# Layer 0's first modulation as plain fp32 products in four 32-column groups, its order of work, and where tiles start in SBUF

## The chip, the core and the metric

The kernel runs on one core of a Trainium2 chip. The metric is device time in microseconds (us) of one execution. Before the change three timed runs gave 1471.29, 1471.39 and 1478.82 us, median 1471.39. The engines are PE (TensorE; PEld is its weight load), DVE (VectorE), ACT (ScalarE), POOL (GpSimd, which issues one kind of DMA here) and SP (which issues the other).

## What is computed

Two layers of a hybrid backbone work on 256 latent and 256 context tokens of width 1024. Only the start of layer 0 is touched by most of the change:

```
mod = silu(c) @ w_mod[0] + b_mod[0]            # one row of 6*1024 for the latents (c), one for the context (c_ctx)
sh1, sc1, gt1, sh2, sc2, gt2 = split(mod, 6)
h  = rms_norm(x,   g_pre_mix[0]) * (1 + sc1)  + sh1
hc = rms_norm(ctx, g_pre_mix[0]) * (1 + csc1) + csh1
rq, rk, ... = split(h @ w_in[0], ...)          # the first 512 columns are rq and rk
```

Everything after it (retention, two attentions, merge, output projection, MLP, both layers) reads `h`.

## The kernel before

Activations are kept transposed, as eight chunks `hT` of 128 channels by 512 tokens (256 in most of layer 1), each as a rounded half and a remainder half in a fast fp32 form (`float32r`; hi and lo). Weights come as raw fp32 tiles of 128 x 1024 (512 KB each) on SP's queue; ACT casts a tile to its hi half (`wh`), DVE subtracts to get the lo half (`wl`), and each product is three matmuls: hi x hi, hi x lo, lo x hi (`mm3`). This goes for nearly every matmul of the kernel.

**The prologue** (function `prologue`, line 243) makes `sh1` and `sc1` of layer 0 and the first projection (512 columns of `w_in`, tiles `pr0` to `pr3`), in four quarters `kp` of 256 channels. A quarter has four pieces of `w_mod` (512 rows x 256 columns each) and one piece of `w_in`; all 20 pieces are loaded in that order (`load`, line 253), at most four ahead of the splits (`PLD`). Line 267 puts the halves of every third piece into the weight buffers and the others into general tiles. The letters of `PLAN` (line 55) are: `c` split pieces up to a number (ACT and DVE), `a` the modulation products of a quarter (line 285), `r` copy of the result row (line 296), `f` turn it into columns and make `sh1`, `sc1` (line 304), `t` transpose the normalised inputs of the quarter, `h` apply `sh1` and `sc1` and split (line 519), `g` the projection's products of the quarter (line 316). The silu vector, split into hi and lo, lies in `msr` as four columns of 128 stationary ones, so a modulation product is one matmul with the hi half of a piece and one with its lo half, each on 128 x 128 stationary and 256 moving columns: 32 matmuls a quarter.

While `Ordered.on` is set (line 325), PE, DVE and ACT instructions stay in the order of the text; after it a scheduler orders them. Waits between engines follow from the tiles. SP and POOL issue their DMAs in the order of the text too. `setup2` (line 1285), the first two tiles of the later vectors' `w_mod` (line 458) and two relative position tables (line 806) are POOL's, and nothing but a free tile holds them back.

**The other five vectors of layer 0 and all of layer 1** (`mod_dve`, line 401) are made on DVE: eight tiles of `w_mod` are scaled and added up (`acc`); the first addition reads the bias from the constant tile `brow`.

**SBUF.** General tiles are 4096 bytes a partition (pool `sp`, 31 of them), small ones 2048 (`tp`), weight halves 1056 numbers, 4224 bytes, in three buffers each (line 221). Two pad tiles (lines 114 and 120) set where the pools start. The built program puts general, small and raw tiles 256 bytes past a multiple of 512; the `wh` buffers 256, 384 and 0 past one, the `wl` buffers 128, 256 and 384.

Of the kernel before, what the change touches and what calls it, by code (L numbers as in the profile page):

```python
# [9 lines left out]
F32 = mybir.dt.float32  # L10
# [20 lines left out]
MLB = 2  # L31
NT = 8
NB2 = 5
C1 = 0
WR = 3
WH = 3
WLD = 3
# [10 lines left out]
XLATE = True  # L48
END = ((0, 0), (1, 0))
ORD = ((0, 4, 5), (0, 4, 8))  # L50
RW = 2
PLD = 4
# [29 lines left out]
def kernel(  # L82
# [121 lines left out]
    brow = const.tile([128, 2, 512], F32, tag="brow", name="brow")  # L204
# [36 lines left out]


    def prologue():
        pr = []
        M = {}
        raw, rdy = {}, {}
# [3 lines left out]
        mi = (0, 5, 10, 15)  # L250
        gi = (4, 9, 14, 19)

        def load(n):
            while len(raw) < min(n, len(wts)):
                i = len(raw)
                ap, k, *_ = wts[i]
                t = S("pr", F32) if i % RW else wrp.tile([128, 2, 512], F32, tag="wr", name="pr")
                raw[i] = t
                st["hold_sp"] = nc.sync.dma_start(
                    out=t.rearrange("p a b -> p (a b)").rearrange("p (k n) -> p k n", k=k), in_=ap)  # L260

        def cut(n):
            while len(rdy) < min(n, len(wts)):
                i = len(rdy)
                load(i + PLD)
                t, k = raw[i], wts[i][1]
                hi = wtile(whp, "wh", "pwh").rearrange("p (a b) -> p a b", a=2) if i % 3 == 0 else S("pwh")
                lo = wtile(wlp, "wl", "pwl").rearrange("p (a b) -> p a b", a=2) if i % 3 == 0 else S("pwl")
                st["hold_act"] = s_.copy(hi, t)
                st["hold"] = tt(lo, t, f(hi), ALU.subtract)  # L270
                rdy[i] = [u.rearrange("p a b -> p (a b)").rearrange("p (k n) -> p k n", k=k) for u in (hi, lo)]

        def init():
            msr = S("msr")
            v_.tensor_copy(msr[:, 0, :], brow[:, 0, :])
            v_.tensor_copy(msr[:, 1, :], brow[:, 0, :])
            msr = msr.rearrange("p a b -> p (a b)").rearrange("p (k m) -> p k m", k=8)
            v_.tensor_copy(msr[:, :, 0:2], cs)
            tt(msr[:, :, 2:4], cs, f(msr[:, :, 0:2]), ALU.subtract)
            M["msr"] = msr  # L280
            for n_ in ("sh1", "sc1"):
                st[0, n_] = smp.tile([128, 8, 2], F32, tag=n_, name=n_, bufs=2)
            pr.extend(mmt(f"pr{i}") for i in range(4))

        def mod(kp):
            ps = att("modps")
            for i in range(4):
                v, hf = i // 2, i % 2
                w = rdy[mi[kp] + i]
# [4 lines left out]
            M["ps", kp] = ps  # L294

        def row(kp):
            s_.copy(st["r5", kp][0:4, :], M["ps", kp][0:4, :])

        def bias(kp):
            r5 = st["r5", kp] = T("r5")  # L300
            nc.gpsimd.dma_start(out=r5[4:5, :].rearrange("o (v n) -> o v n", v=2),
                                in_=b_mod[0:1, 0:2 * D].rearrange("o (v n) -> o v n", v=2)[:, :, 256 * kp:256 * kp + 256])

        def fin(kp):
            r5 = st.pop(("r5", kp))
            pt = att("pm")
            for j in range(4):
                t_.matmul(pt[:, 2 * j:2 * j + 2], r5[0:5, 128 * j:128 * j + 128], sel[0:5, 18:20],
                          start=True, stop=True)
            p3 = pt[:, 0:8].rearrange("p (j e) -> p j e", e=2)  # L310
            hs = slice(2 * kp, 2 * kp + 2)
            v_.tensor_copy(st[0, "sh1"][:, hs, :], p3[:, 0:2, :])
            for s in range(2):
                stt(st[0, "sc1"][:, hs, s], p3[:, 2:4, s], 1.0, gp[:, 0, hs], ALU.add, ALU.mult)

        def gemm(kp):
            w_ = rdy[gi[kp]]
            for k in range(2):
                for i in range(4):
                    kc = 2 * kp + k  # L320
                    w = slice(128 * i, 128 * i + 128)
                    mm3(pr[i], (w_[0][:, k, w], w_[1][:, k, w]), hpair(kc, 512), kc == 0, kc == 7)

        def go(ws):
            Ordered.on = True
            load_x(4)
            load(PLD)
            for kp in range(2):
                bias(kp)
            init()  # L330
            sq = [pre_sq(0)]
            pre_xn(0, sq[0])
            sq.append(pre_sq(1))
            cut(C1)
            pre_xn(1, sq[1])
            for kp, plan in enumerate(PLAN):
                for c in plan.replace("_", " ").split():
                    o, n = c[0], int(c[1:])
                    if o == "c":
                        cut(n)  # L340
                    elif o == "a":
                        mod(n)
                    elif o == "r":
                        row(n)
                    elif o == "t":
                        ph = [pre_tr(n, s) for s in range(2)]
                    elif o == "f":
                        fin(n)
                        if n < 2:
                            bias(n + 2)  # L350
                    elif o == "h":
                        h32 = [T("h32") for _ in range(2)]
                        for j in range(2):
                            for s in range(2):
                                pre_h(0, 0, n, s, ph[s], (j,), h32[s])
                    elif o == "g":
                        gemm(n)
# [43 lines left out]
    def mod_dve(l, vec, streams):  # L401
# [53 lines left out]
        def step(kc):  # L455
            def go(ws):
                w = mrp.tile([128, 2, 512], F32, tag="mr", name="mr")
                nc.gpsimd.dma_start(  # L458
                    out=w, in_=w_mod[l, 128 * kc:128 * kc + 128, vec * D:vec * D + D].rearrange("p (a n) -> p a n", a=2))
                if kc == 0:  # L460
                    nc.gpsimd.dma_start(out=brow[0:1], in_=b_mod[l:l + 1, vec * D:vec * D + D].rearrange("o (a n) -> o a n", a=2))
                for s in streams:
                    if kc == 0:
                        st["acc", s] = S("acc", F32)
                    a = st["acc", s]
                    stt(a, w, cs[:, kc, s:s + 1], brow if kc == 0 else a, ALU.mult, ALU.add)
            return go

        fins = [fin1, fin2] if gate else [fin1, fin2, fin3]
# [257 lines left out]
    def attn_units(l, n, kind):  # L727
# [22 lines left out]
        def s1(hs, qb):  # L750
# [51 lines left out]
            def go():  # L802
                if na and qb == 0:
                    for h in hs:
                        bt = st["bt", h] = btp.tile([128, 384], F32, tag="bt", name="bt")
                        nc.gpsimd.dma_start(out=bt, in_=relb[l, h])
                context() if qb == 2 else latent()

            return go
# [464 lines left out]
    def setup():  # L1274
# [4 lines left out]
        v_.memset(brow, 0.0)  # L1279
# [5 lines left out]
    def setup2():  # L1285
# [7 lines left out]
        v_.tensor_copy(selr, sel4[0:4])  # L1293
        v_.memset(onesf, 1.0)
        v_.tensor_copy(ones, onesf)
        v_.tensor_copy(oneh[:, 0, :], brow[:, 0, 0:128])
        v_.tensor_copy(oneh[:, 1, :], brow[:, 0, 0:128])
        v_.tensor_copy(oneh[:, 0, 0:1], onesf[:, 0:1])
        v_.tensor_copy(oneh[:, 1, 1:2], onesf[:, 0:1])

# [202 lines left out]
```

## Time and profile before

| what | us |
|---|---|
| timed runs | 1471.29, 1471.39, 1478.82; median 1471.39 |
| the profiled execution | 1478.93 |
| its span, first to last instruction | 1477.2 |
| PE matmuls busy | 1427.6 (97%) |
| DVE, ACT busy | 1079.4 (73%), 747.1 (51%) |
| first product of the projection `pr` starts | 31.07 |
| first product of the next step (`pB`) starts | 72.69 |

Times in rows are us from the start of the span. A matmul's busy time is longer than the distance to the next start, because matmuls are pipelined; this text counts from start to start. The profiled execution lies 7.5 us above the median of the timed runs.

### The profile page before, as it was taken

Reading aid. Unit: us, or ns where it says so; the run is one execution under the profiler, and the core shown is the slowest. Engines: PE = TensorE matmul, PEld = TensorE weight load, DVE = VectorE, ACT = ScalarE, POOL = GpSimd, SP = SyncE. Lnnn points to the kernel's source line nnn. Section 1 sums busy time; section 2 is a strip of 40 time slices with the busy share of each in tenths; the row PEclk is TensorE's granted clock in tenths of the full one; section 3 lists DMA queues with packets and bytes.
Section 4 is the critical chain, followed back from the end, with each engine's and each line's share of the span. In section 5 each row is a group of like instructions: output and inputs, shape, how many; then the busy total and the mean of one; then the engine's idle time right before and its main releaser. Section 6 shows DMA issues by size and latency. Waiting matters only on the chain. (4 is left out here: it accounts for less than half of the span.)

```text
span 1477.2 us, 20910 instructions
## 1 busy us (share of the span) xinstructions
PE 1427.6 (97%) x7926; PEld 1212.9 (82%) x7926; DVE 1079.4 (73%) x1999; ACT 747.1 (51%) x1259; POOL 67.8 (5%) x131
## 2 busy tenths in 40 slices
PE   4999999999999999999999999999999999799997
PEld 4878788877788889988888887788889999699886
DVE  5785797787998669967755647986877886766544
ACT  5563565554323347625335155665546655576542
POOL 2000000000110000100001100000000000000000
PEclk9999999999999999999999999999999999899999
DMA  8622121222566556846546647443233445387653
GB/s 287 197 72 72 44 72 58 83 70 91 171 188 183 157 200 174 251 144 188 159 135 218 198 119 235 144 124 95 72 94 107 150 140 189 113 227 215 209 185 119
DMA packets 231957, 219.64 MB, mean 149 GB/s; under 512 B 7652, under 2 KB 188956, under 8 KB 231856
## 3 DMA queue, kind: packets, MB, share of 16 engines
q1 hardware_dynamic: 217856, 170.42, 37.4%
q0 software_dynamic: 14000, 47.88, 10.6%
q8 instruction: 62, 1.02, 0.3%
q14 instruction: 39, 0.32, 0.1%
HBM read 217.22 MB, written 1.05 MB: 148 GB/s over the span
## 5 line engine op out<-in xcount | busy, mean ns | idle before, releaser
L73 PE MATMUL ps<-hT,wh 128*128 128x256 f32 (+1 forms) x2480 | 602.4, 335 | 1.6 <-ACT wh L73 1.6
L73 ACT CAST wh<-wr 128x1024 fp32r<-128x1024 f32 x295 | 309.2, 1051 | 449.9 <-PE ps L73 180.9
L73 DVE TENSOR_TENSOR wl<-wr,wh 128x1024 fp32r<-128x1024 f32 x295 | 359.7, 1223 | 211.7 <-ACT wh L73 211.4
L73 PEld LDWEIGHTS ps<-hT,wh 128*128 128x128 f32 x2480 | 419.1, 190 | 55.5 <-issue 6.6
L73 PE MATMUL ps<-hT,wl 128*128 128x256 f32 (+1 forms) x1240 | 415.2, 335 | 5.1 <-DVE wl L73 4.9
L73 PEld LDWEIGHTS ps<-hT,wl 128*128 128x128 f32 x1240 | 234.9, 189 | 29.2 <-DVE wl L73 6.1
L73 PE MATMUL pO<-wh,u 128*128 128x512 f32 x768 | 241.7, 394 | 0.0
L73 PEld LDWEIGHTS pO<-wh,u 128*128 128x128 f32 x768 | 144.1, 188 | 33.7
L73 DVE SCALAR_TENSOR_TENSOR acc<-mr,cs,acc 128x1024 f32<-128x1024 f32 x112 | 141.2, 1282 | 28.9 <-DMA mr<-in_w_mod_dram 28.4
L73 PE MATMUL pO<-wl,u 128*128 128x512 f32 x384 | 151.2, 394 | 0.2 <-DVE wl L73 0.2
L73 PEld LDWEIGHTS pO<-wl,u 128*128 128x128 f32 x384 | 72.1, 188 | 16.6 <-DVE wl L73 0.6
L73 PE MATMUL pB<-wh,hT 128*128 128x512 f32 x256 | 82.9, 394 | 0.0
L458 POOL DMA_DIRECT2D mr<-in_w_mod_dram x80 | 42.6, 533 | 647.4 <-DVE acc L73 618.5
L73 PE MATMUL pO<-wh,yT 128*128 128x512 f32 x192 | 60.3, 393 | 0.0
L73 PEld LDWEIGHTS pB<-wh,hT 128*128 128x128 f32 x256 | 48.1, 188 | 10.6
L73 DVE TENSOR_TENSOR PT<-pt,PT 128x512 fp32r<-128x512 f32 x80 | 51.5, 682 | 2.8 <-ACT PT L73 2.2
L73 PE MATMUL pB<-wl,hT 128*128 128x512 f32 x128 | 50.3, 393 | 0.0
L73 ACT CAST PT<-pt 128x512 fp32r<-128x512 f32 x80 | 43.2, 599 | 8.5 <-PE pt L73 6.5
L73 PE MATMUL pt<-ident,P 128*128 128x128 f32 x320 | 42.0, 273 | 0.8 <-DVE P L73 0.6
L73 PEld LDWEIGHTS pO<-wh,yT 128*128 128x128 f32 x192 | 35.9, 188 | 8.2
L73 DVE TENSOR_TENSOR u<-rl,u 128x256 fp32r<-128x256 f32 (+1 forms) x71 | 36.7, 517 | 7.4 <-ACT u L73 7.4
L73 DVE TENSOR_SCALAR P<-P,su 128x512 f32<-128x512 f32 (+1 forms) x96 | 40.3, 440 | 1.6
(261 smaller groups left out, 1909.6 us busy)
## 6 DMA issues: line engine op xcount, KB each, us to landing
wr<-in_w_m_dram SPq DMA_DIRECT2D x143, 512.0 KB, 4.5
wr<-in_w_in_dram SPq DMA_DIRECT2D x104, 512.0 KB, 3.7
mr<-in_w_mod_dram POOLq DMA_DIRECT2D x80, 512.0 KB, 4.5
wr<-in_w_br_dram SPq DMA_DIRECT2D x24, 512.0 KB, 3.4
wr<-in_w_out_dram SPq DMA_DIRECT2D x24, 512.0 KB, 3.7
pr<-in_w_mod_dram SPq DMA_DIRECT2D x16, 512.0 KB, 6.3
bt<-in_relb_dram POOLq DMA_DIRECT2D x16, 192.0 KB, 2.7
X<-in_x_dram SPq DMA_DIRECT2D x4, 512.0 KB, 4.9
```

What stands on the lines that cost most here:

```text
L73: ins = call(*a, **k)
L458: nc.gpsimd.dma_start(out=w, in_=w_mod[l, 128 * kc:128 * kc + 128, vec * D:vec * D + D].rearrange("p (a n) -> p a n", a=2))
```

## The change

**The modulation products** read the raw fp32 pieces: no cast, no subtraction. The silu vector lies in `csz` as two columns of 32 per chunk; the four 128-row chunks of a piece go to four groups of 32 output columns (`ps[32 * k:...]`, 256 moving columns each), 16 matmul calls a quarter instead of 32 matmuls. `row` adds a bias tile on DVE, where ACT copied before; `fin` reads all 128 rows and a selector that adds the four groups. Only the four pieces of `w_in` are split, into the weight buffers.

**Loads.** All 20 pieces are issued at once, into general tiles and three raw ones. The bias rows are POOL's first loads after three constants. POOL then copies one number of piece 14 (`late`), and `setup2`, the later vectors' tiles and the position tables come behind that copy. `brow` is a general tile made anew for each vector, cleared by POOL.

**Order.** The products of quarter n come after the modulation of quarter n+1 from quarter 1 on. Five fp32 matmuls on a zero tile stand at PE's start.

**Places.** `PAD`, `PAD2` and the weight tiles' width (1152 numbers, 4608 bytes) change: general, small and raw tiles start at multiples of 2048 bytes, weight halves at multiples of 512.

```diff
-PAD, PAD2 = 16, 16
-PLAN = ["c4 t0 a0 c5 r0 f0 h0 c9 g0 c13",
-        "a1 t1 r1 c14 f1 h1 c18",
-        "a2 r2 c19 g1 t2 f2 h2",
-        "a3 t3 r3 c20 f3 h3 g2"]
+PLAN = "t0 a0 c0 r0 f0 d0 h0 g0 a1 r1 t1 c1 f1 d1 h1 a2 r2 t2 c2 f2 d2 h2 g1 a3 r3 t3 c3 f3 d3 h3 g2"
+GATE = 14
+PAD, PAD2, WP = 200, 272, 1152
+WARM = 5
...
-        t = pool.tile([128, 1056], F32R, tag=tag, name=name)
+        t = pool.tile([128, WP], F32R, tag=tag, name=name)
...
+        def load():
+            for i, (ap, k, *_) in enumerate(wts):
+                t = wrp.tile([128, 2, 512], F32, tag="wr", name="pr") if i % 5 == 4 and i < 15 else S("pr", F32)
                 raw[i] = t
+                st["hold_sp"] = nc.sync.dma_start(out=flat(t, k), in_=ap)
+                if i == GATE:
+                    st["late"] = nc.gpsimd.tensor_copy(out=late, in_=t[:, 0, 0:1])
...
         def init():
+            w, zero = att("warm"), T("zero")
+            v_.memset(zero, 0.0)
+            for _ in range(WARM):
+                t_.matmul(w, zero[:, 0:128], zero, start=True, stop=True)
+            t = S("csz", F32)
+            v_.memset(t, 0.0)
...
         def mod(kp):
-                    for p in range(2):
-                        t_.matmul(ps[:, 256 * v:256 * v + 256], M["msr"][:, 4 * hf + k, :], w[p][:, k, :],
-                                  start=(hf == 0 and k == 0 and p == 0), stop=(hf == 1 and k == 3 and p == 1))
+                    t_.matmul(ps[32 * k:32 * k + 32, 256 * v:256 * v + 256], M["csz"][:, 4 * hf + k, :], w[:, k, :],
+                              start=(hf == 0), stop=(hf == 1))
         def row(kp):
-            s_.copy(st["r5", kp][0:4, :], M["ps", kp][0:4, :])
+            r = M["r", kp] = T("r5")
+            tt(r, M["ps", kp], M["bias"][kp // 2][:, kp % 2, :], ALU.add)
...
-            with tc.issue_after(st["hold"].ins):
+            with tc.issue_after(st["hold"].ins), tc.issue_after(st["late"].ins):
                 setup2()
...
+                with tc.issue_after(st["late"].ins):
                     nc.gpsimd.dma_start(
                         out=w, in_=w_mod[l, 128 * kc:128 * kc + 128, vec * D:vec * D + D].rearrange("p (a n) -> p a n", a=2))
+                    if kc == 0:
+                        M["b"] = S("brow", F32)
+                        nc.gpsimd.memset(M["b"], 0.0)
+                        nc.gpsimd.dma_start(out=M["b"][0:1], in_=b_mod[l:l + 1, vec * D:vec * D + D].rearrange("o (a n) -> o a n", a=2))
```

PE's program, from its first instruction to the first products of the projection, before (`ph` transposes, `modps` modulation, `pm` is `fin`, `pr` the projection; numbers are buffers; 30 more rows of `modps` are left out):

```order
L73 MATMUL ph<-ident,X 128x128 x8
L73 MATMUL modps<-pwh,msr 128x256
L73 MATMUL modps<-pwl,msr 128x256
...
L73 MATMUL pm<-sel,r_138 128x2 x4
L73 MATMUL pr_149<-hT,pwh 128x512 x2
L73 MATMUL pr_149<-hT,pwl 128x512
```

The same place now, and on to the second quarter's modulation and the third's (15 rows of `pr` are left out):

```order
L69 MATMUL warm<-zero 128x512 x5
L69 MATMUL ph<-ident,X 128x128 x8
L69 MATMUL modps<-pr,csz 32x256 x16
L69 MATMUL pm<-csz,r_276 128x2 x4
L69 MATMUL pr_195<-hT,pwh 128x512 x2
...
L69 MATMUL modps<-pr,csz 32x256 x16
L69 MATMUL ph<-ident,X 128x128 x8
L69 MATMUL pm<-csz,r_345 128x2 x4
L69 MATMUL modps<-pr,csz 32x256 x16
```

The 32 matmuls of a quarter are 16 calls that read the raw piece, the run-up stands ahead of the first transposes, and the third quarter's modulation stands ahead of the second quarter's products.

DVE's program between the normalisation of the context and the second group of splits, before (`pwl` a lo half, `sh`, `sc` the columns of `fin`, `h` and `hT` step `h`):

```order
L73 TENSOR_SCALAR X<-X,py 128x1024 x2
L73 TENSOR_TENSOR pwl<-pr,pwh 128x1024 x5
L73 COPY sh_147<-pm 128x4
L73 SCALAR_TENSOR_TENSOR sc_148<-pm,gp 128x2 x2
L73 CAST hT<-h_283 128x256
L73 TENSOR_TENSOR hT<-h_283,hT 128x256
...
L73 TENSOR_TENSOR pwl<-pr,pwh 128x1024 x9
```

And now:

```order
L69 TENSOR_SCALAR X<-X,py 128x1024 x2
L69 TENSOR_TENSOR r_276<-modps,bias 128x512
L69 COPY sh_193<-pm 128x4
L69 SCALAR_TENSOR_TENSOR sc_194<-pm,gp 128x2 x2
L69 TENSOR_TENSOR pwl<-pr,pwh 128x1024
L69 CAST hT<-h_288 128x256
L69 TENSOR_TENSOR hT<-h_288,hT 128x256
```

Sixteen of 20 splits are gone; the one of the quarter stands between `sc` and the first cast of `hT`, and the addition of the bias stands ahead of `sh`.

## Rows read from the trace of the kernel before

**Rows 1.** The page's busy time, share and instructions of each engine.
```profile
PE 1427.6 (97%) x7926; PEld 1212.9 (82%) x7926; DVE 1079.4 (73%) x1999; ACT 747.1 (51%) x1259; POOL 67.8 (5%) x131
```

**Rows 2.** Waits of PE, whole run: waiter, tile, releaser: us, times, longest.
```profile
PE ph L73 <- DVE X L73: 14.2, 4, 10.4
PE ps L73 <- DVE wl L73: 4.9, 3, 2.7
```

**Rows 3.** Stretches: length, busy us of each engine, clock, DMA share, GB/s.
```profile
10.38:31.06 20.68, 12.58 (x48) 10.33 (x48) 11.01 (x29) 8.55 (x12) 1.77 (x4) 1.00 1.03 372
31.06:38.63 7.57, 7.57 (x24) 6.03 (x25) 7.50 (x11) 6.96 (x8) 0.00 (x0) 1.00 0.40 133
38.63:48.33 9.70, 9.70 (x82) 9.51 (x80) 6.65 (x14) 5.24 (x8) 0.00 (x0) 1.00 0.99 337
48.33:61.67 13.34, 13.34 (x90) 11.91 (x88) 9.41 (x20) 8.14 (x13) 0.00 (x0) 1.00 0.43 133
61.67:72.69 11.02, 11.02 (x50) 9.12 (x49) 9.99 (x37) 6.16 (x11) 1.01 (x2) 1.00 0.42 126
```

**Rows 4.** PE's timeline, quarter 0: start, length, tile, count, [idle before].
```profile
16.04 0.90 PE L73 MATMUL ph<-ident,X 128*128 128x128 f32 x3 [0.18 <-DVE X L73]
...
27.29 1.86 PE L73 MATMUL pm<-sel,r 5*128 5x2 f32 x8 [0.66 <-ACT r L73]
31.07 1.26 PE L73 MATMUL pr<-hT,pwh 128*128 128x512 f32 x2 [1.91 <-DVE hT L73]
...
33.83 1.05 PE L73 MATMUL pr<-hT,pwh 128*128 128x512 f32 x2
```

**Rows 5.** PE's timeline, quarter 1 to the end of the prologue.
```profile
38.63 0.28 PE L73 MATMUL modps<-pwh,msr 128*128 128x256 f32 x1
...
42.46 1.03 PE L73 MATMUL ph<-ident,X 128*128 128x128 f32 x8
43.42 1.05 PE L73 MATMUL pm<-sel,r 5*128 5x2 f32 x8
44.40 0.39 PE L73 MATMUL modps<-pwh,msr 128*128 128x256 f32 x1
...
48.33 0.62 PE L73 MATMUL pr<-hT,pwh 128*128 128x512 f32 x2
...
53.65 0.40 PE L73 MATMUL pr<-hT,pwl 128*128 128x512 f32 x1
62.48 0.62 PE L73 MATMUL pr<-hT,pwh 128*128 128x512 f32 x2
...
72.46 0.39 PE L73 MATMUL pr<-hT,pwl 128*128 128x512 f32 x1
72.69 0.39 PE L73 MATMUL pB<-wh,hT 128*128 128x512 f32 x1
```

**Rows 6.** ACT's timeline: the third and fourth input tile, the first piece.
```profile
8.10 1.06 ACT L73 ACTIVATE xj<-X 128x1024 f32<-128x1024 f32 x1 [0.35 <-DMA X<-in_xc_dram]
...
11.60 1.06 ACT L73 ACTIVATE xj<-X 128x1024 f32<-128x1024 f32 x1 [2.34 <-DMA X<-in_xc_dram]
...
13.89 1.04 ACT L73 CAST pwh<-pr 128x1024 fp32r<-128x1024 f32 x1 [1.15 <-DMA pr<-in_w_mod_dram]
```

**Rows 7.** DVE's groups from 0 to 72.69: count | busy, mean ns | idle before.
```profile
L73 DVE TENSOR_TENSOR pwl<-pr,pwh 128x1024 fp32r<-128x1024 f32 x20 | 23.5, 1220 | 7.9 <-ACT pwh L73 7.8
...
L73 DVE MEMSET brow<- 128x1024 f32 x1 | 0.9, 912 | 1.0 <-PEq L1492 1.0
```

**Rows 8.** PE's timeline: products on two different halves of the rows.
```profile
283.02 0.97 PE L73 MATMUL sl<-nk,nq 64*128 64x512 f32 x6
283.92 0.73 PE L73 MATMUL ps<-hT,wh 128*128 128x512 f32 x2
```

**Rows 9.** PE's groups by form, whole run: count | busy, mean ns.
```profile
L73 PE MATMUL ps<-hT,wh 128*128 128x512 f32 x1136 | 362.4, 398 | 0.0
...
L73 PE MATMUL ps<-hT,wl 128*128 128x512 f32 x568 | 226.3, 398 | 0.0
```

More of the change, by code (lines that the diff above doesn't have):

```diff
@@ L33 @@
 NB2 = 5
-C1 = 0
 WR = 3
@@ L203 @@
     cs = const.tile([128, 8, 2], F32, tag="cs", name="cs")
-    brow = const.tile([128, 2, 512], F32, tag="brow", name="brow")
+    late = const.tile([128, 1], F32, tag="late", name="late")
     ones = const.tile([128, 128], F32R, tag="ones", name="ones")
@@ L249, in prologue @@
         wts = md(0) + gm(0) + md(1) + gm(1) + md(2) + gm(2) + md(3) + gm(3)
[L250 to L257, printed above, removed]
-                raw[i] = t
-                st["hold_sp"] = nc.sync.dma_start(
-                    out=t.rearrange("p a b -> p (a b)").rearrange("p (k n) -> p k n", k=k), in_=ap)
@@ L262, in cut @@
[L262 to L271, printed above, removed]
@@ new lines, in cast, with cut, bias @@
+        def cast(kp):
+            hi[kp] = wtile(whp, "wh", "pwh").rearrange("p (a b) -> p a b", a=2)
+            st["hold_act"] = s_.copy(hi[kp], raw[5 * kp + 4])
+        def cut(kp):
+            lo = wtile(wlp, "wl", "pwl").rearrange("p (a b) -> p a b", a=2)
+            st["hold"] = tt(lo, raw[5 * kp + 4], f(hi[kp]), ALU.subtract)
+            rdy[kp] = [flat(u, 2) for u in (hi[kp], lo)]
+        def bias():
+            M["bias"] = [S("bias", F32) for _ in range(2)]
+            for i, t in enumerate(M["bias"]):
+                v_.memset(t, 0.0)
+                for kp in range(2):
+                    c = 512 * i + 256 * kp
+                    nc.gpsimd.dma_start(
+                        out=t[0:2, kp, :].rearrange("o (v n) -> o v n", v=2),
+                        in_=b_mod[0, 0:2 * D].partition_broadcast(2).rearrange("o (v n) -> o v n", v=2)[:, :, c:c + 256])
@@ new lines, in init @@
+        def init():
+            w, zero = att("warm"), T("zero")
[3 more added lines that the diff above has]
+            t = S("csz", F32)
+            v_.memset(t, 0.0)
+            M["csz"], M["selp"] = t[:, 0, 0:256].rearrange("p (k m) -> p k m", k=8), t[:, 1, 0:2]
+            v_.tensor_copy(M["csz"][:, :, 0:2], cs)
+            for j in range(4):
+                r = slice(32 * j, 32 * j + 2)
+                v_.tensor_copy(M["selp"][r, :], ident[r, r])
@@ L285, in mod @@
         def mod(kp):
-            ps = att("modps")
+            ps = M["ps", kp] = att("modps")
             for i in range(4):
                 v, hf = i // 2, i % 2
-                w = rdy[mi[kp] + i]
+                w = flat(raw[5 * kp + i], 4)
                 for k in range(4):
-                    for p in range(2):
-                        t_.matmul(ps[:, 256 * v:256 * v + 256], M["msr"][:, 4 * hf + k, :], w[p][:, k, :],
-                                  start=(hf == 0 and k == 0 and p == 0), stop=(hf == 1 and k == 3 and p == 1))
-            M["ps", kp] = ps
+                    t_.matmul(ps[32 * k:32 * k + 32, 256 * v:256 * v + 256], M["csz"][:, 4 * hf + k, :], w[:, k, :],
+                              start=(hf == 0), stop=(hf == 1))
         def row(kp):
-            s_.copy(st["r5", kp][0:4, :], M["ps", kp][0:4, :])
[L299 to L302, printed above, removed]
+            r = M["r", kp] = T("r5")
+            tt(r, M["ps", kp], M["bias"][kp // 2][:, kp % 2, :], ALU.add)
         def fin(kp):
-            r5 = st.pop(("r5", kp))
+            r = M.pop(("r", kp))
             pt = att("pm")
             for j in range(4):
-                t_.matmul(pt[:, 2 * j:2 * j + 2], r5[0:5, 128 * j:128 * j + 128], sel[0:5, 18:20],
-                          start=True, stop=True)
+                t_.matmul(pt[:, 2 * j:2 * j + 2], r[:, 128 * j:128 * j + 128], M["selp"], start=True, stop=True)
             p3 = pt[:, 0:8].rearrange("p (j e) -> p j e", e=2)
@@ L326, in go @@
             load_x(4)
-            load(PLD)
-            for kp in range(2):
-                bias(kp)
+            bias()
+            load()
             init()
@@ L333, in go @@
             sq.append(pre_sq(1))
-            cut(C1)
             pre_xn(1, sq[1])
[L336 to L357, printed above, removed]
+            ph = {}
+            for c in PLAN.split():
+                o, n = c[0], int(c[1:])
+                if o == "c":
+                    cast(n)
+                elif o == "d":
+                    cut(n)
+                elif o == "a":
+                    mod(n)
+                elif o == "r":
+                    row(n)
+                elif o == "t":
+                    ph[n] = [pre_tr(n, s) for s in range(2)]
+                elif o == "f":
+                    fin(n)
+                elif o == "h":
+                    h32 = [T("h32") for _ in range(2)]
+                    for j in range(2):
+                        for s in range(2):
+                            pre_h(0, 0, n, s, ph[n][s], (j,), h32[s])
+                elif o == "g":
+                    gemm(n)
             Ordered.on = False
             gemm(3)
-            with tc.issue_after(st["hold"].ins):
+            with tc.issue_after(st["hold"].ins), tc.issue_after(st["late"].ins):
                 setup2()
@@ L457, in go @@
                 w = mrp.tile([128, 2, 512], F32, tag="mr", name="mr")
[L458 to L461, printed above, removed]
+                with tc.issue_after(st["late"].ins):
+                    nc.gpsimd.dma_start(
+                        out=w, in_=w_mod[l, 128 * kc:128 * kc + 128, vec * D:vec * D + D].rearrange("p (a n) -> p a n", a=2))
+                    if kc == 0:
+                        M["b"] = S("brow", F32)
+                        nc.gpsimd.memset(M["b"], 0.0)
+                        nc.gpsimd.dma_start(out=M["b"][0:1], in_=b_mod[l:l + 1, vec * D:vec * D + D].rearrange("o (a n) -> o a n", a=2))
                 for s in streams:
@@ L805, in go @@
                         bt = st["bt", h] = btp.tile([128, 384], F32, tag="bt", name="bt")
-                        nc.gpsimd.dma_start(out=bt, in_=relb[l, h])
+                        with tc.issue_after(st["late"].ins):
+                            nc.gpsimd.dma_start(out=bt, in_=relb[l, h])
                 context() if qb == 2 else latent()
@@ L1295, in setup2 @@
         v_.tensor_copy(ones, onesf)
-        v_.tensor_copy(oneh[:, 0, :], brow[:, 0, 0:128])
-        v_.tensor_copy(oneh[:, 1, :], brow[:, 0, 0:128])
+        for i in range(2):
+            v_.tensor_scalar_mul(out=oneh[:, i, :], in0=onesf, scalar1=0.0)
         v_.tensor_copy(oneh[:, 0, 0:1], onesf[:, 0:1])
```

17 lines of the change are left out of this document (4 added, 13 removed).

## The prediction

> **What bounds the kernel now.** I read first the busy shares: PE matmuls 97% of the span, DVE and ACT far below [rows 1]. Time is lost only where PE waits or where its products are longer than they must be. The table of PE's waits, second, shows where it waits: the transposes `ph` for the normalised inputs `X`, 14.2 us in four waits, the longest 10.4; the largest later entry, products `ps` behind a lo half, is 4.9 [rows 2]. So the waiting that this change can touch is the prologue's. Third, the table by stretches: from 10.38 to 31.06 PE is busy 12.58 of 20.68 us and DMA is at its limit (1.03, 372 GB/s); from 31.06 to 72.69 PE is busy all the time (7.57 + 9.70 + 13.34 + 11.02), also in the stretch where DMA is at 0.99 [rows 3]. After 31.07 only less PE work can shorten the prologue; before it, what counts is how late the inputs, pieces and splits come.
>
> The clock column prints 1.00 for all these stretches, but durations tell two levels apart: the eight passes of `fin` take 1.86 at 27.29 and 1.05 at 43.42, two 512-column products 1.05 at 33.83 and 0.62 at 48.33 [rows 4, 5]. [...] PE comes to the upper level only after the gapless run that begins at 31.07; in the 61% busy stretch ahead of it it did not [rows 3, 4].
>
> **The change part by part.** The sum is made against the profiled execution, 1478.93 us, and then moved to the median.
>
> *Start of the projection.* The third input tile starts its square at 8.10, the context's second tile at 11.60 after a wait of 2.34 for its load [rows 6]. Earlier tiles come about 1.5 us apart, which is also 512 KB (0.524 MB) at 372 GB/s, 1.41 us [rows 3]. POOL's 2 MB of tiles and tables, which load at the same time before, now stand behind piece 14; so I put this tile at 9.6, 2.0 us earlier. The last transposes, which need it and run from 16.04 to 16.94 [rows 4], end then near 14.8. The first piece is cast at 13.89 now [rows 6]; the four of quarter 0 would land at 11.1, 12.5, 13.9 and 15.3, with no cast or subtraction between them and PE. POOL's bias rows are a few KB; ahead of the pieces they cost nothing that I can see.
>
> *The modulation products.* Before, quarter 1 has 32 passes from 38.63 to 42.46, 3.83 us, 0.12 each at the upper level [rows 5]. Now there are 16 calls. How often does PE pass for an fp32 call? `fin` has four fp32 calls and shows x8, two passes per call [rows 4, 5], so 32 passes of 256 columns again. What one takes is bounded from both sides. Below: the four column groups run fully beside each other, and a pass takes as long as 512 float32r columns, 0.23 us: 32 x 0.23 / 4 = 1.84 us a quarter. Above: no overlap, a full load of weights ahead of each pass (0.12, from `fin`, whose eight passes of two columns take 0.98 between 43.42 and 44.40 [rows 5], so are nearly all load) and the same 0.23: 32 x 0.35 = 11.2. The nearest row on overlap is the score products, on two halves of the rows: six in 0.90 us from 283.02 to 283.92, 0.15 each [rows 8], against 0.23 for one alone, so two groups gave 1.5 times, not 2. Four groups at 0.23 with an overlap of about 2 come to 32 x 0.12 = 3.84. I take that value: no gain in the products themselves.
>
> [...]
>
> *From the products to g0.* Transposes end at 14.8, products 3.84 us later at 18.6. The bias addition on DVE (512 elements from PSUM) I put at 0.7, near ACT's copy and the 0.66 that `fin` waited for it [rows 4]; `fin` takes 0.98; the stretch from its end (31.07 - 1.91 = 29.16) to the first product is 1.91 [rows 4]; and on DVE one split of 23.5 / 20 = 1.2 us [rows 7] now stands between `sc` and the first cast of `hT`. 18.6 + 0.7 + 1.0 + 1.9 + 1.2 = 23.4, with a little for queues 23.5. It was 31.07: 7.6 us less. The other 16 splits freed 19 us of DVE and about as much of ACT, but PE had no gap there, so I count them at nothing.
>
> *g0.* Its 24 products took 31.07 to 38.63, 7.56 us, the first half at the lower level [rows 3 to 5]; the same 24 take 48.33 to 53.65 plus one more, 5.55 [rows 5]. The five run-up products (fp32, 512 columns) start near 5.3, after DVE's clearing of two tiles (0.9 each by [rows 7]), and cost nothing: PE waits until 10.38 anyway [rows 2]. Whether they leave the clock high until g0 no row shows, since the transposes that follow are sparse. If it is high, g0 gains 2.0. If it is low, quarter 0's products take up to 2.9 more, `fin` 0.9 more, and g0 stays: 5.8 us lost of my sum. I take the upper level, since the low one needs gaps after a run like that of 31.07, and keep 5.8 for the range.
>
> *After g0.* The order a1, r1, t1, f1, a2, g1, a3, g2 has the same PE work: 41.6 us in all less 2.0. The last pieces must be there: at 1.41 us each from 9.6 on, the 19th and 20th land near 36 to 38; the held-back 2 MB, let go near 31, can push them by 2 / 0.372 = 5.4 us to about 43, and the products that need them (a3) begin 11.0 + 1.9 + 3.8 us ahead of `pB`, at about 46. Hidden; if it were not, up to 5 us. POOL's tiles come some 25 us later than before, but the first vector made of them is not read before the output projection, behind all of `pB`. The bias tile, cleared by POOL for each vector, takes the place of one that DVE cleared once, 0.9 us [rows 7]: nothing. Sum for the prologue: 7.6 + 2.0 = 9.6, minus 0.1 for three bias additions that PE meets no more than before: 9.5 us. `pB` starts near 63.
>
> *Places of tiles.* The same 512-column products run at two speeds. The second group of projection products, whose moving halves lie in the weight buffers, at other offsets from a multiple of 512 bytes than the stationary tiles, takes 23 steps from 48.33 to 53.65: 231.3 ns each. The third and fourth group, whose halves lie in general tiles at the same offset as the stationary ones, takes 44 steps from 62.48 to 72.46: 226.8 ns [rows 5]. The difference, 4.5 ns, is at the same clock and without waits. The later products `ps` read their halves from the weight buffers as the slow ones do; there are 1136 + 568 [rows 9], and 288 alike under `br`. After the change everything starts at a multiple of 512, so I expect the fast speed: 1992 x 4.5 = 9.0 us, at 97% busy nearly all of it in the end time. Bounds: the other 1824 products of this width (`pO`, `pB`, with weights stationary) may gain as much, 8.2 us more, or nothing (I take nothing, as no grouped row separates them); and if offset zero is a bad place in itself, 4.5 ns more on 1992, 9 us lost.
>
> [...]
>
> *Sum.* 9.5 + 9.0 = 18.5: 1478.93 - 18.5 = 1460.4 for a like execution. It stands 7.5 above the median; from the median, 1471.39 - 18.5 = 1452.9, so 1453.
>
> **The rivals.** One: places bring nothing; only the prologue's 9.5 is left, 1462. For it: 231 against 227 may come from DMA writes, 133 GB/s against 126 in the two stretches [rows 3]; against it, these shares are nearly alike.
>
> Two: column groups don't overlap, and the weight load stands in the open: 0.12 + 0.12 a pass, 7.7 us a quarter, four times 3.84 more: 1453 + 15.4 = 1468. For it `fin`'s passes, nearly all load [rows 5]; against it, a 32-column load is a quarter of the full one.
>
> Three, slower than before: loads in the open and fp32 columns at half rate, 0.35 a pass, 11.2 us a quarter, four times 7.36 more: 1453 + 29.4 = 1482. Place: the `modps` rows; it makes the kernel slower than before once a quarter takes more than 3.84 + 18.5 / 4 = 8.5 us. For it, that no row shows a wide fp32 product; against it, two overlapping groups of [rows 8].
>
> Four, better: groups fully beside each other (1.84 a quarter, 8 us less) and, or, `pO` and `pB` gaining too (8 less): 1437 to 1445, say 1442.
>
> That the change does not do what it says would be: the places come out of step for the halves, or the clock stays low in quarter 0 (both priced above).
>
> **How the numbers follow.** About 0.5%, 7.4 us, is what a measurement here can tell from no change: faster means below 1464.0, slower above 1478.8. Forecast 0.45 (own range 1446 to 1460, with the low clock, late loads, and part of the gains of rival four); rival one 0.20, rival two 0.10, rival three 0.08, rival four 0.17. Faster: the forecast, rival four, and three quarters of rival one (a quarter of it, with the low clock, lies at 1464 to 1468): 0.45 + 0.17 + 0.15 = 0.77. Same: 0.05 + 0.10 = 0.15. Slower 0.08. The range 1439 to 1468 leaves out rival three, the edge of rival two and the best end of rival four, together under 0.2.
>
> **What would show it.** `pB` starting near 63; first `pr` near 23.5, behind a `pwl` split; a quarter of `modps` from first to last start 3.8 us (1.8: four groups together; 7.7 or 11: rivals); the first two 512-column products of g0 at 0.62, not 1.05, for the clock; no wait of PE for a piece after g0; and later `ps` groups at 227 ns a product, not 231 to 233. The forecast is wrong if `modps` is longer than 8.5 us, if `ps` keeps its mean, or if PE waits for the last pieces near 46.

## The result, and the profile after

The changed kernel takes 1462.24 us (median of five, 1458.71 to 1464.21) against 1471.39 beside it (1470.72 to 1478.82): ratio 0.992, 95% interval 0.9898 to 0.9941, so 0.6 to 1.0% faster. 1453 was forecast, range 1439 to 1468. The sign and the range held; about half of the forecast 18.5 us came, or three quarters of it by the later runs of the kernel before (medians 1476.28 of 29, 1475.07 of 15, 1476.81 of 17).

The two profiled executions, 1478.93 and 1458.71, differ by 20.2 us. The page's busy times of the changed kernel, for [rows 1]:

```profile
span 1456.9 us, 20916 instructions
PE 1409.7 (97%) x7936; PEld 1200.3 (82%) x7936; DVE 1065.3 (73%) x1991; ACT 729.7 (50%) x1239; POOL 77.8 (5%) x142
```

PE's timeline of the prologue, for [rows 4, 5] (start, length, tile, count, idle before):

```profile
5.72 7.06 PE L69 MATMUL warm<-zero 128*128 128x512 f32 x10 [5.72 <-DVE zero L69]
...
14.28 0.55 PE L69 MATMUL ph<-ident,X 128*128 128x128 f32 x3 [0.33 <-DVE X L69]
14.76 1.93 PE L69 MATMUL modps<-pr,csz 128*32 128x256 f32 x32
17.51 1.05 PE L69 MATMUL pm<-csz,r 128*128 128x2 f32 x8 [0.81 <-DVE r L69]
20.94 1.25 PE L69 MATMUL pr<-hT,pwh 128*128 128x512 f32 x2 [2.38 <-DVE hT L69]
...
28.25 1.93 PE L69 MATMUL modps<-pr,csz 128*32 128x256 f32 x32
30.12 1.09 PE L69 MATMUL ph<-ident,X 128*128 128x128 f32 x8
...
37.09 1.02 PE L69 MATMUL pm<-csz,r 128*128 128x2 f32 x8 [2.08 <-DVE r L69]
37.97 1.09 PE L69 MATMUL pr<-hT,pwh 128*128 128x512 f32 x2
...
49.74 0.62 PE L69 MATMUL pr<-hT,pwh 128*128 128x512 f32 x2
...
59.94 0.39 PE L69 MATMUL pB<-wh,hT 128*128 128x512 f32 x1
```

The first `pB` starts at 59.94, 12.75 us earlier than in [rows 5]. A quarter's modulation takes 28.25 to 30.12, 1.87 us, where 3.84 were forecast: 0.058 a pass, the lower bound of the prediction's range. The first `pr` comes at 20.94, not 23.5. But `fin` of quarter 2 waits 2.08 for the bias addition, and g0 and g1 begin with pairs of 1.25 and 1.09 us, where a pair of the third group takes 0.62. The stretches of the two groups (length, busy us of PE, PEld, DVE, ACT, POOL; granted clock, DMA share, GB/s), for [rows 3]:

```profile
20.94:28.25 7.31, 7.31 (x24) 5.54 (x24) 1.67 (x5) 1.05 (x1) 0.00 (x0) 0.77 1.08 389
37.97:45.25 7.28, 7.28 (x27) 5.55 (x26) 3.94 (x12) 2.95 (x6) 0.00 (x0) 0.77 0.90 353
```

Their mean granted clock is 0.77: 0.55 and 0.54 up to 24.74 and 41.71, 1.00 behind. In g0 four products from 22.00 to 23.70 start 0.43 us apart and 14 from 24.74 to 27.93 start 0.23 apart. Each stretch takes 7.3 us, where 24 products at the upper level take 24 x 0.227 = 5.45. PE had idled 2.38 and 2.08 us shortly before. The input side went as forecast: ACT's timeline shows the fourth tile's square at 9.73 (11.60 in [rows 6], 9.6 forecast).

```profile
9.73 1.06 ACT L69 ACTIVATE xj<-X 128x1024 f32<-128x1024 f32 x1 [0.48 <-DMA X<-in_xc_dram]
```

From the first `pB` to the end of the span the profiles have 1477.2 - 72.69 = 1404.5 and 1456.9 - 59.94 = 1397.0 us: 7.5 less, 9.0 forecast. The two stretches, of before and of the change:

```profile
72.69:1477.20 1404.51, 1373.43 (x7639) 1165.99 (x7637) 1029.94 (x1872) 707.09 (x1203) 57.72 (x109) 0.99 0.47 144
59.94:1456.90 1396.96, 1361.47 (x7639) 1166.35 (x7637) 1030.06 (x1867) 708.38 (x1204) 68.10 (x120) 0.99 0.48 145
```

PE is busy 12.0 us less and idle 4.4 us more (31.1 and 35.5). So two things of opposite sign are in the 7.5. First, products are shorter. PE's groups by form, for [rows 9]:

```profile
L69 PE MATMUL ps<-hT,wh 128*128 128x512 f32 x1136 | 360.0, 396 | 1.8 <-ACT tg L69 1.0 <-DVE z L69 0.9
...
L69 PE MATMUL ps<-hT,wl 128*128 128x512 f32 x568 | 222.9, 392 | 0.0
```

Busy times overlap, so a stretch without waits is better: 192 products `pO` of the MLP of layer 0. Here are the second of them and the `ps` behind them, 191 steps, of before and of the change:

```profile
712.11 0.40 PE L73 MATMUL pO<-wl,u 128*128 128x512 f32 x1
...
756.40 0.63 PE L73 MATMUL ps<-hT,wh 128*128 128x512 f32 x2
```

```profile
695.80 0.39 PE L69 MATMUL pO<-wl,u 128*128 128x512 f32 x1
...
739.12 0.61 PE L69 MATMUL ps<-hT,wh 128*128 128x512 f32 x2
```

44.29 / 191 = 231.9 ns and 43.32 / 191 = 226.8 ns: the forecast's two speeds, but on `pO` too, which the sum had at nothing.

Second, waits came back. PE's waits that grew, for [rows 2], and the 300 us up to the same product at the end of layer 0's MLP, of before and of the change:

```profile
PE pO L69 <- DVE wl L69: 3.3, 2, 2.8
PE pm L69 <- DVE r L69: 2.9, 2, 2.1
PE pr L69 <- DVE hT L69: 2.4, 1, 2.4
```

```profile
615.40:915.40 300.00, 299.09 (x1303) 241.39 (x1302) 192.82 (x194) 113.93 (x151) 28.47 (x54) 1.00 0.57 179
```

```profile
600.00:900.00 300.00, 295.96 (x1307) 242.64 (x1305) 195.19 (x197) 115.10 (x154) 33.45 (x59) 0.99 0.59 180
```

PE is idle 0.9 us there before and 4.0 after. DVE's timeline of the changed kernel at the longest of these waits, and PE's behind it:

```profile
886.40 1.28 DVE L69 SCALAR_TENSOR_TENSOR acc<-mr,cs,acc 128x1024 f32<-128x1024 f32 x1 [0.46 <-DMA mr<-in_w_mod_dram]
890.30 1.29 DVE L69 SCALAR_TENSOR_TENSOR acc<-mr,cs,acc 128x1024 f32<-128x1024 f32 x1 [2.62 <-DMA mr<-in_w_mod_dram]
891.50 0.68 DVE L69 TENSOR_TENSOR z<-z,pO 128x512 f32<-128x512 f32 x1
892.10 1.22 DVE L69 TENSOR_TENSOR wl<-wr,wh 128x1024 fp32r<-128x1024 f32 x1
```

```profile
893.37 0.50 PE L69 MATMUL pO<-wl,u 128*128 128x512 f32 x1 [2.79 <-DVE wl L69]
...
896.15 0.63 PE L69 MATMUL pO<-wl,u 128*128 128x512 f32 x1
896.58 0.63 PE L69 MATMUL pO<-wh,u 128*128 128x512 f32 x1
```

PE's product behind that `wl` starts at 893.37 after 2.79 us of idle time. Then the clock falls too: eight products from 894.87 to 898.28 start 0.43 us apart and not 0.227, 1.6 us more, and the mean granted clock from 893.37 to 898.50 is 0.67. The lo half stands behind the last two additions of a modulation vector, and the second of these waits 2.62 for its tile. DVE's program order there, before and now:

```
L73 SCALAR_TENSOR_TENSOR acc<-mr,cs,acc 128x1024
L73 TENSOR_TENSOR u<-rl,u 128x512
L73 SCALAR_TENSOR_TENSOR acc<-mr,cs,acc 128x1024
L73 TENSOR_TENSOR wl<-wr,wh 128x1024
L73 TENSOR_TENSOR alo<-acc,ahi 128x1024
L73 TENSOR_TENSOR wl<-wr,wh 128x1024 x2
```

```
L69 TENSOR_TENSOR wl<-wr,wh 128x1024 x2
L69 SCALAR_TENSOR_TENSOR acc<-mr,cs,acc 128x1024 x2
L69 TENSOR_TENSOR z<-z,pO_7851 128x512
L69 TENSOR_TENSOR wl<-wr,wh 128x1024
```

Before, the three lo halves at the end come behind the last addition and without another between them; now two come ahead of the last two additions and the third waits for both. The scheduler made this order; the diff sets no order here. But the diff does change how these vectors get their bias (`brow`), besides the earlier end of the prologue, and no run separates which of the two moved the order.

### The profile page after: what moved, and what is told of

Its sections match the earlier page's. It is cut to its first block, busy times and chain, and to the rows that moved or that the text cites. A ratio compares the mean times of both kernels' runs of the same rounds, so it can differ in the third digit from the quotient of the medians.

```text
span 1456.9 us, 20916 instructions
## 1 busy us (share of the span) xinstructions
PE 1409.7 (97%) x7936; PEld 1200.3 (82%) x7936; DVE 1065.3 (73%) x1991; ACT 729.7 (50%) x1239; POOL 77.8 (5%) x142
## 3 DMA queue, kind: packets, MB, share of 16 engines
HBM read 217.23 MB, written 1.05 MB: 150 GB/s over the span
## 4 chain that ended last, share of the span: by engine, by line
PE 84%; DVE 8%; DMA 4%; issue 2%; ACT 1%; DVEq 0%; SPq 0%; ACTq 0%; POOLq 0%
PE ps L69 39%; PE pO L69 16%; PE br L69 7%; PE pB L69 6%; DMA mr<-in_w_mod_dram 3%; PE po L69 3%; PE pt L69 2%; DVE wl L69 2%; PE sl L69 2%; PE gkv L69 2%; PE pr L69 1%; PE ro L69 1%; DVE z L69 1%; DVE hT L69 1%; PE ph L69 1%
```

## Experiments

Each ratio is to the kernel before, run beside the experiment on the same chip. The changed kernel was not run beside them: a distance to its 1462.24 us lies between two sets of runs, and its ratio to compare with is 0.992 (0.9898 to 0.9941). "Tail" is the span less the start of the first `pB`, in the profiled execution; it was 1404.5 before and 1397.0 after.

**The kernel before once more.**

> The kernel before, unchanged, once more. Two accounts of why the two profiled executions differ by 20.2 us and the medians by 9.15. Account A: the first profile of before (1478.93) fell in an execution with some 7.5 us of extra waiting that has a place in the trace; then a second profile near 1471 has the same prologue (first pB at 72.7) and the same 512-column products (near 232 ns), and 7 us less somewhere behind it. Account B: the profile of before is typical and the timed runs of before are spread by something that the trace doesn't show; then a second profile at 1471 differs everywhere by 0.5%. Time by both: 1471 or 1478.

1475.23 us (12 runs) against 1476.28; profiled 1478.74. First `pB` at 72.50, tail 1477.0 - 72.50 = 1404.5, the same as in the first profile. That the totals agree is chance. The tail of this profile, and 170 to 190 us of the first profile and of this one:

```profile
72.50:1477.00 1404.50, 1376.51 (x7639) 1167.04 (x7637) 1029.78 (x1872) 706.67 (x1203) 57.74 (x109) 0.99 0.47 144
```

```profile
170.00:190.00 20.00, 20.00 (x93) 15.40 (x92) 16.81 (x39) 10.49 (x16) 0.00 (x0) 1.00 0.10 27
170.00:190.00 20.00, 20.00 (x64) 14.74 (x64) 10.73 (x26) 7.12 (x11) 0.00 (x0) 0.66 0.09 27
```

PE has no gap there in either, yet the granted clock is 1.00 in the first and 0.66 in this one, which falls some 6 us behind and makes it up later, with 28.0 us of idle time in the tail where the first has 31.1. So the accounts are not decided: the second profile did not fall near 1471 either, and 11 of the 61 later runs of the kernel before are as long. What it shows is that a tail from a single profile is good to a few us only, because the clock falls in other places in each of the two. The median of five, 1471.39, lay low: the 61 later runs have medians of 1475 to 1477. The spread goes with the clock: of 29 runs the shortest, 1469.02, had a mean granted clock of 0.991 and the longest, 1482.46, 0.984; correlation -0.87.

**Old places.**

```diff
-PAD, PAD2, WP = 200, 272, 1152
+PAD, PAD2, WP = 16, 16, 1056
```

> The changed kernel with the pads and the width of the weight tiles of before (16, 16, 1056); the instructions of every engine are the same in the same order. Theory P (places set the pace of 512-column products): products go back from 227 to about 232 ns, which is 13.7 us of flow by the two profiles; of it 6 us was given back in waits for late halves, so 7 to 14 us slower than the changed kernel, 1469 to 1476. Rival W (the gain behind the prologue comes from other waits, not places): within 2 us of 1462. The prologue ends near 60 to 61 by both.

1471.23 us (12 runs), 9.0 above the changed kernel, ratio to before 0.9967 (0.9946 to 0.9988). Tail 1469.4 - 61.13 = 1408.3, 11.3 more. The same 191 steps:

```profile
701.54 0.40 PE L69 MATMUL pO<-wl,u 128*128 128x512 f32 x1
...
745.84 0.63 PE L69 MATMUL ps<-hT,wh 128*128 128x512 f32 x2
```

44.30 / 191 = 231.9 ns: exactly the pace of before. (The pads put the general tiles at another offset than before, 288, but all distances between tiles modulo 512 are those of before.) Theory P holds, W falls. With these distances the tail is 3.8 us longer than before's 1404.5. PE is idle 34.4 us of it, against 31.1, so most of the 3.8 is waiting that the change brought.

**128 bytes apart, and 256.**

```diff
-PAD, PAD2, WP = 200, 272, 1152
+PAD, PAD2, WP = 232, 240, 1152      # 128 apart
+PAD, PAD2, WP = 264, 208, 1152      # 256 apart
```

> The changed kernel with general and small tiles 128 bytes past a multiple of 512, the weight halves still at multiples of 512; the order of all instructions is the same. Theory P: every 512-column product reads its moving tile and the next stationary one at places 128 bytes apart and takes 232 to 234 ns, 5 to 7 ns more on 3816 products, 19 to 27 us of flow, some of it hidden by waits: 1474 to 1488. Rival Q (only multiples of 2048, or the first tile's place, count, not the distance of the two): 1462, or no regular step.

> The changed kernel with general and small tiles 256 bytes past a multiple of 512 and the weight halves at multiples of 512; same order of all instructions. Theory M256 (what counts is whether the two tiles lie a multiple of 256 bytes apart): 227 to 228 ns a 512-column product, like the changed kernel, 1460 to 1464. Rival M512 (a multiple of 512 apart is needed): 231 to 233 ns as with 128 apart, 1470 to 1476.

128 apart: 1473.85 us (12 runs), 11.6 above the changed kernel; tail 1474.4 - 61.07 = 1413.3. 256 apart: 1458.76 (4 runs), no worse than the changed kernel; tail 1455.8 - 61.35 = 1394.5. The 191 steps, 128 apart, then 256:

```profile
702.83 0.39 PE L69 MATMUL pO<-wl,u 128*128 128x512 f32 x1
...
747.21 0.62 PE L69 MATMUL ps<-hT,wh 128*128 128x512 f32 x2
```

```profile
694.01 0.39 PE L69 MATMUL pO<-wl,u 128*128 128x512 f32 x1
...
737.33 0.61 PE L69 MATMUL ps<-hT,wh 128*128 128x512 f32 x2
```

44.38 / 191 = 232.4 and 43.32 / 191 = 226.8 ns. Over the whole tail PE is busy 1381.2 us at 128 and 1360.7 at 256, with the same instructions in the same order. M256 holds where all products have one distance: 0 and 256 are fast, 128 is slow. Neither the multiple of 2048 nor that of 512 is needed for it.

It does not hold product by product where distances are mixed. In the kernel before, by its places, `wh` lies 0, 128 or 256 bytes and `wl` 384, 0 or 128 past the other tile, so four of nine products are 128 apart (modulo 256). Were these alone slow, the mean would be 226.8 + 4/9 x 5.6 = 229.3 ns, and it is 231.9: even if the four take the 232.4 of the run with 128, the other five, 0 or 256 apart, take (9 x 231.9 - 4 x 232.4) / 5 = 231.5 on average, an estimate from the two means. So the distance within one product is not the whole cause; what else counts in such a stream, these runs leave open.

**No run-up.**

```diff
-WARM = 5
+WARM = 0
```

> The changed kernel without the five fp32 products at PE's start. Theory R (the run-up lifts the clock of quarter 0's modulation): its 32 passes take 3.7 us and not 1.87, fin 1.9 and not 1.05, first pB 2 to 3 us later, 1464 to 1465. Rival: the transposes lift the clock, or the end of the first products waits for pieces anyway; then within 0.5 us.

1462.03 us (6 runs), as with it. The trace is clearer:

```profile
10.32 0.48 PE L69 MATMUL ph<-ident,X 128*128 128x128 f32 x1 [10.32 <-DVE X L69]
...
14.93 2.99 PE L69 MATMUL modps<-pr,csz 128*32 128x256 f32 x32
18.75 1.05 PE L69 MATMUL pm<-csz,r 128*128 128x2 f32 x8 [0.82 <-DVE r L69]
```

The modulation takes 2.99 and not 1.93. The last three transposes ahead of it take 0.90 and not 0.55, `fin` behind it 1.05 as with the run-up, so the pace rises inside it. `pB` starts at 61.89, 1.95 later. Theory R is right in kind and too large (3.7, and 1.9 for `fin`, were expected). Two microseconds are below what these times tell, and the tails of single profiles differ by as much.

**One column group.**

```diff
-                    t_.matmul(ps[32 * k:32 * k + 32, ...], ..., start=(hf == 0), stop=(hf == 1))
+                    t_.matmul(ps[0:32, ...], ..., start=(hf == 0 and k == 0), stop=(hf == 1 and k == 3))
```

> The changed kernel with all 16 modulation calls of a quarter on one group of 32 output columns, accumulating one after the other, and fin over 32 rows; bytes, calls, passes and order are the same. Theory G (the four groups run beside each other; alone a pass of 256 fp32 columns takes 0.23 us): modps of a quarter goes from 1.87 to 32 x 0.23 = 7.4 us, 5.5 more in each of four quarters, of which quarter 0 may hide a little behind late pieces: first pB near 80, time near 1482 to 1485. Rival H (a pass takes 0.06 by itself, groups or not): 1.9 a quarter, 1462. Between, 0.12 a pass: 3.8 a quarter, pB near 68, 1470.

1473.62 us (10 runs), 11.4 above the changed kernel (the profiled executions, 1474.77 and 1458.71, differ by 16.1). PE's timeline and its first `pB`:

```profile
33.27 7.09 PE L69 MATMUL modps<-pr,csz 128*32 128x256 f32 x32
40.30 1.09 PE L69 MATMUL ph<-ident,X 128*128 128x128 f32 x8
...
77.04 0.39 PE L69 MATMUL pB<-wh,hT 128*128 128x512 f32 x1
```

7.03 us a quarter, 0.22 a pass, 5.16 more than with four groups, and `pB` is 17.1 later. Theory G holds: a pass of 256 fp32 columns costs what 512 float32r columns cost (0.22 and 0.227 us here), and four groups run 7.03 / 1.87 = 3.8 times faster than one.

**g1 ahead of fin 2.**

```diff
-... a2 r2 t2 c2 f2 d2 h2 g1 a3 ...
+... a2 r2 t2 c2 g1 f2 d2 h2 a3 ...
```

> The changed kernel with the projection products of quarter 1 ahead of fin 2 instead of behind it (modulation and transposes of quarter 2 stay ahead). [...]

Without the wait of 2.08 at `fin` 2 and the 1.8 us of g1's slow start `pB` would come near 56, an estimate from 59.94. It starts at 59.79, as with the change: the wait is gone at `fin` 2 and stands at `fin` 3, and slow pairs stand in g2 (1.06 us at 48.73 and at 50.01).

```profile
40.45 0.95 PE L69 MATMUL pm<-csz,r 128*128 128x2 f32 x8
...
46.26 1.02 PE L69 MATMUL pm<-csz,r 128*128 128x2 f32 x8 [1.98 <-DVE r L69]
```

So the edit moved the wait and did not remove it. The median, 1456.92 (4 runs), is still 5.3 below the changed kernel's, with a tail of 1395.3 against 1397.0; the ratios, 0.9884 (0.9863 to 0.9904) and 0.992, overlap in their intervals. That difference is not in the edited stretch. Of the 1.7 us between the tails 1.1 lie at 140 to 148 us, where the granted clock is 0.79 here and 0.57 in the changed kernel's profile; where the rest comes from the runs don't settle.

**No gate.**

```diff
-                    st["late"] = nc.gpsimd.tensor_copy(out=late, in_=t[:, 0, 0:1])
-            with tc.issue_after(st["hold"].ins), tc.issue_after(st["late"].ins):
+            with tc.issue_after(st["hold"].ins):
...
-                with tc.issue_after(st["late"].ins):
```

> The changed kernel with POOL's loads not held behind piece 14; the four bias loads then come behind the tables and the first vector tile in POOL's queue. Theory L (2 MB of early loads delay inputs and biases): the fourth input tile lands 2 us later, the bias addition of quarter 0 waits, first pr 2 to 5 us later than 20.9, pB 62 to 65, 1464 to 1467. Rival: PE is bound by the order of its own work, pB within 0.5 us of 59.9, 1462.

1467.54 us (6 runs), ratio 0.9947 (0.9925 to 0.9969), which overlaps with the changed kernel's; the trace is clearer, with `pB` at 67.64. ACT's fourth input tile comes at 12.85 and not 9.73, and PE waits for pieces in quarter 0:

```profile
12.85 1.06 ACT L69 ACTIVATE xj<-X 128x1024 f32<-128x1024 f32 x1 [2.01 <-DMA X<-in_xc_dram]
```

```profile
21.40 1.08 PE L69 MATMUL modps<-pr,csz 128*32 128x256 f32 x8 [1.38 <-DMA pr<-in_w_mod_dram]
```

Theory L holds, at 7.7 us of `pB` and not 2 to 5. Three of them are the input (the last transposes start at 17.29 and not 14.28) and 2.1 waits for pieces. Most of the rest is the clock, which is 0.52 from 18.00 to 32.22: `fin` takes 1.86 there and not 1.05.

**The later vectors spread over three steps fewer**, in the changed kernel and in the one before.

```diff
-MLB = 2
+MLB = 5
```

> The changed kernel with the steps of the later modulation vectors spread over three steps fewer of the MLP of layer 0, so that on DVE no addition of a vector stands between the last lo halves of the MLP; the prologue is untouched. Theory B (order on DVE: lo halves queue behind an addition that waits for its load; PE waits 3 to 5 us some 830 to 848 us after the first pB in all four profiles with the changed order, and 0 to 1.1 in the two of before): these waits go, 3 to 5 us less, 1457 to 1459. Rival C (the waits come from the loads themselves, whatever the order): they stay, 1462.

> The kernel before with the vectors spread over three steps fewer, as in the run that did this to the changed kernel. Theory B (the change of order spoilt a place that was good before): the two profiles of before have 0 to 1.2 us of long waits there, so little to win, 0 to 2 us below before. Rival (fewer steps help whatever the order): 5 to 8 us below before, as for the changed kernel.

In the changed kernel: 1453.44 us (4 runs), ratio to before 0.985 (0.9828 to 0.9872); tail 1450.1 - 59.91 = 1390.2, 6.8 less. In the one before: 1473.83 (12 runs), ratio 0.9984 (0.9967 to 1.0); tail 1475.8 - 70.97 = 1404.8, as without the edit. The 300 us at the end of the MLP, in the changed kernel with the edit:

```profile
600.00:900.00 300.00, 300.00 (x1339) 246.93 (x1338) 199.17 (x202) 118.33 (x157) 33.44 (x59) 1.00 0.60 184
```

No idle time is left. Theory B holds: in the kernel before, idle 0 to 0.9 us there, the edit is worth 0 to 5 us by the interval, in the changed kernel more. Of the 6.8 us of the tail 5.0 are idle time of PE (35.5 us without the edit, 30.5 with it). The rest is busy time: 1.6 are the slow products behind the long wait, and 1.1 at 140 to 148 us are none of the edit's doing, since the granted clock is 0.57 there in the changed kernel's profile and 0.79 in this one; about 1 us is lost again elsewhere.

**Both together**, with the split of a quarter's `w_in` piece on DVE ahead of `fin`'s results.

```diff
+PLAN = "t0 a0 c0 r0 d0 f0 h0 g0 a1 r1 t1 c1 d1 f1 h1 a2 r2 t2 c2 d2 g1 f2 h2 a3 r3 t3 c3 d3 f3 h3 g2"
+MLB = 5
```

> The kernel of the run with the vectors spread over fewer steps, and in the prologue the split of each quarter's w_in piece on DVE ahead of fin's results instead of behind them, and g1 ahead of fin 2. Theory D (split behind fin's results holds the first product back): first pr at 19.6 and not 20.8, the wait at fin 3 about 1 us and not 2, pB near 57.5, 2 to 3 us less than that run: 1450 to 1452. Rival: waits move again, pB near 59.8, 1453.

1451.46 us (6 runs, 1448.23 to 1460.25), ratio to before 0.9851 (0.9817 to 0.9885): the fastest version here, though not clearly apart from the one without the new order.

```profile
20.53 0.96 PE L69 MATMUL pr<-hT,pwh 128*128 128x512 f32 x2 [1.98 <-DVE hT L69]
...
45.49 1.02 PE L69 MATMUL pm<-csz,r 128*128 128x2 f32 x8 [1.56 <-DVE r L69]
...
57.35 0.39 PE L69 MATMUL pB<-wh,hT 128*128 128x512 f32 x1
```

`pB` is at 57.35 as expected, but the first product came only 0.4 earlier, not 1.2: the wait for `hT` is 1.98 with the split out of its way and was 2.38 with it, so most of the split had lain beside the chain from `fin` over `h` to `hT`.

## Why the prediction was right or wrong

**Wrong: the start from the median.** The step "from the median, 1471.39 - 18.5" failed. The profile of before was a long run, but no stray: the later medians are 1475 to 1477, and from those the change brings 13 to 15 us. The rest of the distance to the profiles' 20.2 is chance on both sides: 2 to 4 us by which the profile of before lies above those medians, and 3.5 by which the changed kernel's lies below its own.

**Luck: the sum.** The sum for a like execution was 1460.4 and the profiled one took 1458.71. But that is not its terms coming true: 7.9 us in the modulation and 7.3 in `pO` and `pB`, which it did not have, were for the most part lost again in waits and at the lower clock level, which it did not have either. So both mechanisms of rival four came true (1.87 a quarter, `pO` and `pB` faster) without its 1437 to 1445, and the time of rival one, 1462, came true without its mechanism.

**Right in sign, 3.3 us too small: the prologue.** Forecast 9.5, measured 12.75. The failing term is the modulation: 1.87 a quarter and not 3.84, since four column groups run beside each other almost fully (one group alone takes 7.03 a quarter, 3.8 times as long); I had carried the 1.5 of the score products [rows 8] over as 2. Rivals two and three fall with it: `modps` was to take 7.7 or 11. The loads that they put in the open run beside products on the same rows, in the kernel before too: from 31.06 to 38.63 the loads are busy 6.03 of 7.57 us while products on all 128 rows never pause [rows 3]. A 32-column load takes 109 ns on average in the changed kernel and a full one of `fin` 191, so more than a quarter of it; a pass with its load takes 0.058 us. Of the 4 x 1.97 = 7.9 us that the groups won in the modulation, part was lost again: 2.1 at `fin` 2, which the prediction said would not happen ("three bias additions that PE meets no more than before"), and 1.8 each in g0 and g1, which it had put at the upper level. That leaves 2.2 of the 3.3; the last 1.1 are small steps of both signs. The value 5.5 for g0 was wrong; the reason for doubt, sparse work on PE ahead of it, was there. The reason given for the upper level, that the low one needs gaps, does not hold in general: the second profile of before ran at 0.66 from 170 to 190 us without a gap, the changed kernel's at 0.57 from 140 to 148.

**Right: loads.** The fourth input at 9.73 (9.6 forecast), no wait for a piece, run-up hidden: the last transposes start at 14.28 with it and 14.10 without. The gate is worth the 7.7 us of `pB` that its absence cost.

**Right in kind, wrong account: places.** 9.0 forecast, 7.5 in the tail. Counted over all 512-column steps without a gap behind the first `pB`, `ps` and `br` gain 4.2 ns each, 8.3 us, near the 9.0; but `pO` and `pB`, which I had at nothing, gain 4.0 ns each, 7.3 us more. Waits (4.4) and, as far as they were traced, stretches at the lower clock took half of the 15.6 back. By the run with old places the gain is 11.3 and 3.8 were given back. The prediction also has the roles the wrong way round: in `pr` and `ps` the weights are the stationary tiles and `hT` moves, and in `pB` and `pO` the weights move; its sum goes by the distance of the two and does not change. The runs with 128 and 256 bytes have the same instructions in the same order, and 232.4 and 226.8 ns. Rival one falls.

**Missed: the order far from the change.** With the change the scheduler orders DVE's additions and lo halves differently 830 us later, for 4.0 us of idle PE, where it was 0.9, and 1.6 us more at the lower clock. Whether the earlier end of the prologue or the new `brow` moved it is not shown. The prediction looked at order only in the prologue. It also called 4.9 us the largest later wait of PE; the table has `ph` behind `z` with 10.6, and it is still there with 10.9.

## What to carry to other kernels

Before placing a change's gain against a median, see how far the medians of other runs lie from it; a profile is a better base only when its stretches, and not just its total, come again in a second one. Where matrix products run back to back, read their pace from start to start over a long stretch and compare tiles by their distance in bytes: here all tiles 128 apart cost 2.5% and all 256 apart nothing, and a mixture cost 2.2% on average, by the estimate above also on products 0 or 256 apart. After any change of timing compare the order of every engine to the end of the program, above all what stands ahead of the operation that the busiest engine waits for.

## What the runs showed of the hardware

- Matmuls on 512 columns take 226.8 ns with all moving and stationary tiles 0 or all 256 bytes apart (modulo 512), 232.4 with all 128 apart, and 231.9 on average with the mixed places of before (191 steps from `pO` on in each run).
- An fp32 pass of 256 columns takes 0.22 us alone and 0.058 with three other column groups beside it.
- After idle stretches of 2.38 and 2.08 us PE's products in g0 and g1 started 0.43 us apart at first and 0.23 apart later (mean granted clock 0.77 over 7.3 us): 1.8 us lost each, beside the idle time itself. After 2.79 us of idle time at 890 eight products started 0.43 apart, 1.6 us lost. The clock was also low without a gap: 0.66 over 20 us, busy throughout, in one of two profiles of the kernel before, and 0.57 over 8 us in the changed kernel's.
- Executions of one kernel lie 13 us apart (1469.02 to 1482.46), and the mean granted clock, 0.991 to 0.984, goes with it (correlation -0.87).
